# Two transfers for every weight block: a converting one into the first part, an adding one onto its negative

## The chip, the core and the metric

The kernel runs on one core of a Trainium2 chip. The metric is device time in microseconds (us), the median of the runs shown. The core has a matrix engine (PE; PEld is its weight load), a vector engine (DVE), an activation engine (ACT), a general engine (POOL), a sync engine (SP) that here only issues transfers, and 16 DMA engines that carry out what SP, ACT and POOL issue. Each engine works through its own instructions in order.

## The reference

The program is two transformer blocks on 512 tokens of width 1024, in f32. The first has a chunked state-space branch (SSD) of eight groups of heads, a banded attention, a gate and an MLP; the second has a parallel mixer, an attention to a memory and an MLP. What matters here is that nearly all of the work is products with weight matrices, such as

```python
proj = h @ w_in[l]
f = jnp.square(jax.nn.relu(h @ w_mlp_in[l])) @ w_mlp_out[l]
```

with the inner dimension of such a product 1024 or a multiple of it.

## The kernel before

**The products.** PE multiplies float32r, a rounded form of f32. To keep precision, a weight is held as two parts, `hi` (the weight rounded to float32r) and `lo` (what the rounding left), and an activation as two parts likewise. A product is then three matmuls: hi by hi, hi by lo and lo by hi (lines 266 to 268 in `cm`, channel-major; 284 to 286 in `tm`, token-major). For every 128 rows of weights the third matmul of `cm` is the first to need `lo`.

**The stream of blocks.** Weights come as a stream of some 140 blocks (`Unit`), nearly all of 1 MB: 128 partitions by 8 rows of 256 columns. `load` issues the transfer of a block into `raw`, from SP (line 129). `split` makes the parts, in two halves: ACT copies `raw` into `whi`, which rounds (line 140), and DVE subtracts `whi` from `raw` into `wlo` (line 141). `raw`, `whi` and `wlo` have two buffers each. `use` is called where a block's products begin: it sees that this block is split, and then `ahead` splits the next block and loads the one after that. So a transfer has about two blocks' time, and the split one block's time, before PE needs them.

**The order.** A tile framework records the program and arranges each engine's instructions by a schedule, so an instruction can stand earlier on its engine than the Python order says, but never runs before its inputs are there and its buffer is free.

**Around the change in the MLPs.** Each MLP has four quarters of four blocks of the first matrix (`f1`) and four of the second (`f2`). After each half of an `f1` block, ACT makes `relu` (line 1161) and its square `ua_h` (1162), POOL makes the square again in f32, `fsq` (1164), and DVE takes the difference as `ua_l` (1165). In the SSD stage POOL masks exponents (`e`, line 666), adds (`w`, 670; `xd`, 694 and 697) and issues the small transfers of `rh` and `lh` (561, 562, 626, 628), which go from f32 into float32r tiles.

Of the kernel before, what the change touches and what calls it, by code (L numbers as in the profile page):

```python
# [9 lines left out]
F32 = mybir.dt.float32  # L10
# [6 lines left out]
P = 128  # L17
# [5 lines left out]
WN = 2048  # L23
# [20 lines left out]
# columns of w_in  # L44
Z0, XBC0, DT0, Q0, K0, V0, G0 = 0, 2048, 6144, 6208, 7232, 7488, 7744
# columns of w_in_2
U0, VM0, OP0, IF0 = 0, 512, 1024, 1536

# columns of the packed constants
# [3 lines left out]
def packed_constants():  # L53
    """Constants that depend on shapes alone: the identity and its mirror image, the rotary
    frequencies, the one-hot of the relative position buckets, and the fixed rows of the products
    that make the exponents of the decays."""
# [11 lines left out]
    # rows 0..7 choose the chunk, rows 64..127 the pair that a token is in  # L68
# [4 lines left out]
    # rows 8..15 choose the head, rows 64..127 hide the pairs of tokens that a direction doesn't see  # L73
# [11 lines left out]
def body(ctx, tc, a, out, dbg=None):  # L85
# [26 lines left out]
    # ---------------------------------------------------------------- weights, as a stream of blocks  # L112
    win, win2 = a["w_in"][0], a["w_in_2"][0]

    class Unit:
        """A block of weights [128, kt, n], split into two parts of float32r whose sum it is."""

        def __init__(self, kt, n, loads, flat=None):
            self.kt, self.n, self.loads, self.flat = kt, n, loads, flat
            self.raw = self.hi = None  # L120
# [4 lines left out]
        def load(self):  # L125
            if self.raw is None:
                self.raw = self.view(wp.tile([P, WN], F32, name=nm("raw"), tag="raw", bufs=2))
                for dst, src in self.loads:
                    self.last = nc.sync.dma_start(out=dst(self.raw), in_=src)

        def split(self):
            if self.hi is None:
                self.load()
                self.hi = self.view(wp.tile([P, WN], F32R, name=nm("whi"), tag="whi", bufs=2))
                self.lo = self.view(wp.tile([P, WN], F32R, name=nm("wlo"), tag="wlo", bufs=2))
                n = self.flat or self.n
                for c in range(0, n, max(P, n // 2)):
                    e = min(n, c + max(P, n // 2))
                    sl = (slice(None), slice(c, e)) if self.flat else (slice(None), slice(None), slice(c, e))
                    A.copy(self.hi[sl], self.raw[sl])  # L140
                    V.tensor_tensor(out=self.lo[sl], in0=self.raw[sl], in1=self.hi[sl].bitcast(F32), op=ALU.subtract)  # L141
# [11 lines left out]
    def use(key, lag=False):  # L153
        """The unit; the next one is split at once or, with lag, where ahead() says."""
# [5 lines left out]
    def ahead(key, *behind):  # L160
        """The next unit being split, behind the given instructions, and the one after it on its way."""
# [9 lines left out]
    def evac_first(key, evac, *args):  # L171
        """evac, with the next unit's split behind the first of it on each engine."""
# [78 lines left out]
    # ---------------------------------------------------------------- helpers  # L251
    def cm(key, act, evac, parts=1):
        """Steps of a channel-major product: evac(j, psum) for each 128 columns of the unit, each in
        one step or more."""
# [19 lines left out]
    def tm(key, act, evac, ntile=NT):  # L274
        """Steps of a token-major product: evac(t, psum) for each 128 tokens."""
# [20 lines left out]
    def weave(main, side):  # L296
        """The steps of both lists, each list spread evenly."""
# [13 lines left out]
    def split_from(src, hi, lo, gain=None):  # L311
        """hi + lo = src * gain (a column of gains), both float32r."""
# [7 lines left out]
    def inv_rms(dst, ssq, n, width):  # L320
        """dst = (ssq / n + eps) ** -0.5 for [128, width] columns."""
# [3 lines left out]
    def token_sums(ssq, tag="t"):  # L325
        """Sums over the partitions of [128, 512], token-major in PSUM [128, 4]."""
# [5 lines left out]
    def bcast_tokens(r, tag="t"):  # L332
        """[128, 4] token-major -> PSUM [128, 512] on every partition."""
# [5 lines left out]
    # ---------------------------------------------------------------- persistent tiles  # L339
# [17 lines left out]
    # ---------------------------------------------------------------- block 1, first norm  # L357
# [12 lines left out]
    # the tensor engine's clock is at its full rate when the first inputs are here  # L370
# [34 lines left out]
    # ---------------------------------------------------------------- parameters, as columns  # L405
# [34 lines left out]
    # ---------------------------------------------------------------- dt and the decays  # L440
# [14 lines left out]
    # what the products for the exponents take: see ssd_exponents  # L455
# [4 lines left out]
    def dt_evac(_, po):  # L460
        """Rows (half, direction, head), two chunks of tokens in each half."""
# [17 lines left out]
        # cumulative sums of dt * a in each chunk, forwards and backwards  # L479
# [13 lines left out]
        # cs in two float32r parts, by way of DRAM, where the heads of a group are one row  # L493
# [8 lines left out]
        # the logarithm of dt, less cs, in two parts too  # L502
# [11 lines left out]
        # token-major: exp(cs) and dt * exp(tot - cs)  # L514
# [14 lines left out]
        def late():  # L529
# [8 lines left out]
            # the decay over a whole chunk, on every partition; step k takes chunk k and chunk 3 - k  # L538
# [25 lines left out]
    # ---------------------------------------------------------------- block 1, SSD branch  # L564
# [22 lines left out]
    class Group:  # L587
        """The SSD branch of one group of four heads."""
# [5 lines left out]
        # products, convolution and layouts  # L594
# [27 lines left out]
        # rows of the products for the exponents  # L622
# [32 lines left out]
        def exponents(self, c):  # L655
            """dt[s] exp(cs[l] - cs[s]) of both directions: cs[l] comes from rows 0..7,
# [1092 lines left out]
```

## Time and profile before

| | |
|---|---|
| median of 3 runs | 1943.59 us (1941.83 to 1944.87) |
| span of the profiled execution | 1939.5 us |
| PE busy | 1868.0 us (96%) |
| DVE / ACT / POOL busy | 1083.4 / 856.8 / 482.8 us |
| DMA queue of SP | 24.8% of the 16 engines' span |

The span runs from the first to the last instruction of the profiled execution; the page gives no other time of that execution. The difference of span and median, 4.1 us, is what lies around the span. A matmul's end is modelled, since matmuls are pipelined, so the distance from one matmul's start to the next is what one costs. Timeline rows give the start, then the duration, in us.

### The profile page before, as it was taken

How to read it: one execution, taken by the hardware profiler on the slowest of the kernel's cores; microseconds unless marked ns; L12 is line 12 of the kernel's file. 1: busy time of each engine (PE TensorE's matmuls, PEld its weight loads, DVE VectorE, ACT ScalarE, POOL GpSimd, SP SyncE). 2: the span in 40 equal slices, each digit the busy share in tenths (PEclk: the TensorE clock that was granted, in tenths of full speed). 3: DMA queues.
4: the chain of work that ended last, by engine and by line, in shares of the span. 5: the costliest groups of instructions: out<-in, count | busy, mean ns of one | idle time of the engine just before them, and what ended most of it. 6: DMA issues, size and time to landing. Idle time of an engine off the chain costs nothing. (4 is left out here: it accounts for less than half of the span.)

```text
span 1939.5 us, 24660 instructions
## 1 busy us (share of the span) xinstructions
PE 1868.0 (96%) x9685; PEld 1541.4 (79%) x9685; DVE 1083.4 (56%) x1751; ACT 856.8 (44%) x1397; POOL 482.8 (25%) x530
## 2 busy tenths in 40 slices
PE   8989999999999999998999999989999999999999
PEld 6878778887887777887888888888877778888887
DVE  7767773777555654537334334667567763334543
ACT  5655652755335665345332323444453543323231
POOL 1544450444202221233011202322110431111020
PEclk9999999999999999999999999999999999999999
DMA  6222122221222221333333332322111213232322
GB/s 174 68 67 67 45 67 87 67 67 44 82 94 82 82 78 66 119 122 109 98 109 98 101 94 89 114 73 74 51 45 65 87 44 108 90 107 87 109 87 65
DMA packets 169377, 164.10 MB, mean 85 GB/s; under 512 B 8742, under 2 KB 165101, under 8 KB 169262
## 3 DMA queue, kind: packets, MB, share of 16 engines
q1 hardware_dynamic: 157322, 151.03, 24.8%
q10 hardware_dynamic: 9444, 9.89, 1.6%
q0 software_dynamic: 2496, 1.61, 0.3%
q8 instruction: 76, 1.25, 0.3%
q14 instruction: 39, 0.32, 0.1%
HBM read 158.26 MB, written 4.23 MB: 84 GB/s over the span
## 5 line engine op out<-in xcount | busy, mean ns | idle before, releaser
L141 DVE TENSOR_TENSOR wlo<-raw,whi 128x1024 fp32r<-128x1024 f32 (+2 forms) x285 | 374.9, 1329 | 277.8 <-ACT whi L140 275.4
L140 ACT CAST whi<-raw 128x1024 fp32r<-128x1024 f32 (+2 forms) x285 | 288.3, 1029 | 408.9 <-PE psg L267 381.1
L266 PE MATMUL psg<-hh,whi 128*128 128x512 f32 (+1 forms) x1016 | 403.0, 397 | 0.8 <-DVE hl L318 0.8
L267 PE MATMUL psg<-hl,whi 128*128 128x512 f32 (+1 forms) x1016 | 400.7, 394 | 0.0
L268 PE MATMUL psg<-hh,wlo 128*128 128x512 f32 (+1 forms) x1016 | 399.3, 393 | 0.0
L266 PE MATMUL psg<-ua_h,whi 128*128 128x512 f32 x800 | 316.5, 396 | 0.5 <-DVE xT L1562 0.5
L267 PE MATMUL psg<-ua_l,whi 128*128 128x512 f32 x800 | 313.4, 392 | 0.0
L268 PE MATMUL psg<-ua_h,wlo 128*128 128x512 f32 x800 | 312.3, 390 | 0.0
L266 PEld LDWEIGHTS psg<-hh,whi 128*128 128x128 f32 (+1 forms) x1016 | 191.0, 188 | 40.5 <-issue 1.2
L268 PEld LDWEIGHTS psg<-hh,wlo 128*128 128x128 f32 (+1 forms) x1016 | 190.7, 188 | 39.7
L267 PEld LDWEIGHTS psg<-hl,whi 128*128 128x128 f32 (+1 forms) x1016 | 190.8, 188 | 38.1 <-DVE hl L315 0.4
L1164 POOL TENSOR_TENSOR fsq<-relu 128x512 f32<-128x512 f32 x64 | 80.9, 1264 | 507.9 <-ACT relu L1161 434.5
L266 PEld LDWEIGHTS psg<-ua_h,whi 128*128 128x128 f32 x800 | 150.1, 188 | 35.4 <-DVE xT L1562 2.4
L267 PEld LDWEIGHTS psg<-ua_l,whi 128*128 128x128 f32 x800 | 150.3, 188 | 32.3 <-DVE ua_l L1165 1.2
L268 PEld LDWEIGHTS psg<-ua_h,wlo 128*128 128x128 f32 x800 | 150.2, 188 | 30.7
L284 PE MATMUL psg<-whi,hh 128*128 128x256 f32 x416 | 121.5, 292 | 2.7 <-ACT sz L608 2.7
L286 PE MATMUL psg<-whi,hl 128*128 128x256 f32 x416 | 121.8, 293 | 0.0
L285 PE MATMUL psg<-wlo,hh 128*128 128x256 f32 x416 | 120.5, 290 | 1.0 <-DVE wlo L141 1.0
L986 POOL TENSOR_TENSOR ssq<-ssq,sq 128x512 f32<-128x512 f32 x42 | 66.4, 1582 | 117.0 <-ACT sq L985 116.0
L1165 DVE TENSOR_TENSOR ua_l<-fsq,ua_h 128x512 fp32r<-128x512 f32 x64 | 47.3, 739 | 79.2 <-POOL fsq L1164 79.2
L284 PEld LDWEIGHTS psg<-whi,hh 128*128 128x128 f32 x416 | 81.5, 196 | 5.9 <-ACT sz L608 4.0
L285 PEld LDWEIGHTS psg<-wlo,hh 128*128 128x128 f32 x416 | 81.4, 196 | 1.6 <-DVE wlo L141 1.2
(560 smaller groups left out, 2910.4 us busy)
## 6 DMA issues: line engine op xcount, KB each, us to landing
raw<-in_w_in_dram SPq DMA_DIRECT2D x37, 1024.0 KB
raw<-in_w_ff_dram SPq DMA_DIRECT2D x32, 1024.0 KB
raw<-in_w_mlp_in_dram SPq DMA_DIRECT2D x16, 1024.0 KB
raw<-in_w_mlp_out_dram SPq DMA_DIRECT2D x16, 1024.0 KB
raw<-in_w_in_dram SPq DMA_DIRECT2D x16, 512.0 KB
raw<-in_w_ssd_out_dram SPq DMA_DIRECT2D x8, 1024.0 KB
raw<-in_w_attn_out_dram SPq DMA_DIRECT2D x4, 1024.0 KB
raw<-in_w_o_dram SPq DMA_DIRECT2D x4, 1024.0 KB
```

The costliest lines, as they stand in the source:

```text
L140: A.copy(self.hi[sl], self.raw[sl])
L141: V.tensor_tensor(out=self.lo[sl], in0=self.raw[sl], in1=self.hi[sl].bitcast(F32), op=ALU.subtract)
L266: T.matmul(o, lhsT=u.hi[:, k, c:e], rhs=xh[k], start=k == 0, stop=False)
L267: T.matmul(o, lhsT=u.hi[:, k, c:e], rhs=xl[k], start=False, stop=False)
L268: T.matmul(o, lhsT=u.lo[:, k, c:e], rhs=xh[k], start=False, stop=k == u.kt - 1)
L284: T.matmul(o, lhsT=xh[k][:, tk], rhs=u.hi[:, k, 0 : u.n], start=k == 0, stop=False)
L285: T.matmul(o, lhsT=xh[k][:, tk], rhs=u.lo[:, k, 0 : u.n], start=False, stop=False)
L286: T.matmul(o, lhsT=xl[k][:, tk], rhs=u.hi[:, k, 0 : u.n], start=False, stop=k == u.kt - 1)
L986: G.tensor_tensor(out=self.t, in0=self.t, in1=q, op=ALU.add)
L1164: G.tensor_tensor(out=f, in0=r, in1=r, op=ALU.mult)
L1165: V.tensor_tensor(out=ua_l[:, m, :], in0=f, in1=ua_h[:, m, :].bitcast(F32), op=ALU.subtract)
```

## The change

The tile `raw` is gone. `load` now issues a transfer straight into `whi`, from POOL, with the conversion to float32r done by the transfer. `split` has ACT write the negative of `whi` into `wlo` (two halves, as before), and then issues from POOL a second transfer of the same weights that adds onto `wlo`. DVE's subtraction is gone. `whi` and `wlo` have three buffers each in place of two, so that the six buffers of a block's size stay six. All else in the diff is comments taken out; lines behind the class move by two.

```diff
         def load(self):
-            if self.raw is None:
-                self.raw = self.view(wp.tile([P, WN], F32, name=nm("raw"), tag="raw", bufs=2))
+
+            if self.hi is None:
+                self.hi = self.view(wp.tile([P, WN], F32R, name=nm("whi"), tag="whi", bufs=3))
                 for dst, src in self.loads:
-                    self.last = nc.sync.dma_start(out=dst(self.raw), in_=src)
+                    self.last = nc.gpsimd.dma_start(out=dst(self.hi), in_=src)
 
         def split(self):
-            if self.hi is None:
+
+            if self.lo is None:
                 self.load()
-                self.hi = self.view(wp.tile([P, WN], F32R, name=nm("whi"), tag="whi", bufs=2))
-                self.lo = self.view(wp.tile([P, WN], F32R, name=nm("wlo"), tag="wlo", bufs=2))
+                self.lo = self.view(wp.tile([P, WN], F32R, name=nm("wlo"), tag="wlo", bufs=3))
...
-                    A.copy(self.hi[sl], self.raw[sl])
-                    V.tensor_tensor(out=self.lo[sl], in0=self.raw[sl], in1=self.hi[sl].bitcast(F32), op=ALU.subtract)
+                    A.activation(self.lo[sl], self.hi[sl].bitcast(F32), AF.Copy, scale=-1.0)
+                for dst, src in self.loads:
+                    nc.gpsimd.dma_start(out=dst(self.lo), in_=src, accum_op=ALU.add)
```

POOL's queue in the first MLP, `f1` blocks of a later quarter, before. It holds the squares alone; the loads are on SP.

```order
L1164 TENSOR_TENSOR fsq_1355_8239<-relu_1354_8236 128x512 [waits Activation_49,Pool_49]
L1164 TENSOR_TENSOR fsq_1358_8270<-relu_1357_8267 128x512 [waits Activation_49,Pool_49]
L1164 TENSOR_TENSOR fsq_1364_8309<-relu_1363_8306 128x512 [waits Activation_49,Pool_49]
L1164 TENSOR_TENSOR fsq_1367_8340<-relu_1366_8337 128x512 [waits Activation_49,Pool_49]
L1164 TENSOR_TENSOR fsq_1373_8379<-relu_1372_8376 128x512 [waits Activation_49,Pool_49]
```

The same place after. Line 143 is the adding transfer, line 130 the converting one; the first number behind a name is the buffer's own, in the order in which the program takes them: `whi_1336` and `wlo_1343` are one block, `whi_1344` and `wlo_1351` the next.

```order
L143 DMA wlo_1335_8612<-in_w_mlp_in_dram 128x8x256 [waits DMASW5_49,PE_49,Activation_49]
L130 DMA whi_1336_8616<-in_w_mlp_in_dram 128x8x256 [waits DMASW6_49,PE_49]
L1166 TENSOR_TENSOR fsq_1334_8609<-relu_1333_8606 128x512 [waits Activation_49,Pool_49]
L1166 TENSOR_TENSOR fsq_1339_8646<-relu_1338_8643 128x512 [waits Activation_49,Pool_49]
L143 DMA wlo_1343_8680<-in_w_mlp_in_dram 128x8x256 [waits DMASW7_49,PE_49,Activation_49]
L130 DMA whi_1344_8684<-in_w_mlp_out_dram 128x8x256 [waits DMASW0_49,PE_49]
L1166 TENSOR_TENSOR fsq_1342_8677<-relu_1341_8674 128x512 [waits Activation_49,Pool_49]
L1166 TENSOR_TENSOR fsq_1347_8714<-relu_1346_8711 128x512 [waits Activation_49,Pool_49]
L143 DMA wlo_1351_8748<-in_w_mlp_out_dram 128x8x256 [waits DMASW1_49,PE_49,Activation_49]
L130 DMA whi_1352_8752<-in_w_mlp_out_dram 128x8x256 [waits DMASW2_49,PE_49]
```

Both transfers of a block now stand between the squares, and the converting transfer of a block stands right behind the adding one of the block before it.

ACT's queue at the same place, before:

```order
L140 CAST whi_1359_8273<-raw_1352_8209 128x8x128 [waits DMAHW0_49,PE_49]
L1161 ACTIVATE relu_1357_8267<-psg_1356_8242 128x512 [waits DVE_49,PE_49]
L140 CAST whi_1359_8273<-raw_1352_8209 128x8x128
L1162 ACTIVATE ua_h_74<-relu_1357_8267 128x512 [waits Activation_49]
L1161 ACTIVATE relu_1363_8306<-psg_1362_8281 128x512 [waits DVE_49,PE_49]
L1162 ACTIVATE ua_h_74<-relu_1363_8306 128x512 [waits Activation_49]
```

and after:

```order
L141 ACTIVATE wlo_1343_8680<-whi_1336_8616 128x8x128 [waits DMASW7_49,DMASW4_49]
L1163 ACTIVATE relu_1338_8643<-psg_1337_8618 128x512 [waits DVE_49,PE_49]
L141 ACTIVATE wlo_1343_8680<-whi_1336_8616 128x8x128
L1164 ACTIVATE ua_h_74<-relu_1338_8643 128x512 [waits Activation_49]
L1163 ACTIVATE relu_1341_8674<-psg_1340_8649 128x512 [waits DVE_49,PE_49]
L1164 ACTIVATE ua_h_74<-relu_1341_8674 128x512 [waits Activation_49]
```

The two halves now enclose the `relu` of a block's first half instead of that of its second half, and the wait for PE (a `whi` buffer to be free) is replaced by waits for transfers.

## Rows read from the trace of the kernel before

**Rows 1.** Page, part 1: busy time, share of the span, instructions of each engine.
```profile
PE 1868.0 (96%) x9685; PEld 1541.4 (79%) x9685; DVE 1083.4 (56%) x1751; ACT 856.8 (44%) x1397; POOL 482.8 (25%) x530
```

**Rows 2.** Who waited for whom: us in total, times, longest.
```profile
ACT whi L140 <- PE psg L267: 381.1, 79, 9.3
DVE wlo L141 <- ACT whi L140: 275.4, 127, 11.1
...
SPq L129 <- DVE wlo L141: 1463.4, 121, 39.2
```

**Rows 3.** Groups by line and form: count | busy us, mean ns | idle before, releaser.
```profile
L141 DVE TENSOR_TENSOR wlo<-raw,whi 128x1024 fp32r<-128x1024 f32 x275 | 368.6, 1354 | 274.5 <-ACT whi L140 274.3
...
L140 ACT CAST whi<-raw 128x1024 fp32r<-128x1024 f32 x275 | 283.6, 1048 | 408.5 <-PE psg L267 381.1 <-issue 11.4 <-PE pse L1226 9.6
...
L712 PE MATMUL pst<-ident,sz 128*128 128x128 f32 x60 | 12.7, 312 | 10.5 <-DVE ua_l L318 5.8 <-DVE sz L707 4.7
```

**Rows 4.** Timeline of ACT over one block of the first MLP.
```profile
998.36 1.05 ACT L140 CAST whi<-raw 128x1024 fp32r<-128x1024 f32 x1 [3.95 <-PE psg L267]
999.31 0.59 ACT L1161 ACTIVATE relu<-psg 128x512 f32<-128x512 f32 x1
...
1009.24 1.05 ACT L140 CAST whi<-raw 128x1024 fp32r<-128x1024 f32 x1 [3.95 <-PE psg L267]
```

**Rows 5.** One load of 1 MB: SP's timeline row, then the stretch; last columns clock, DMA share, GB/s.
```profile
1002.68 0.37 SPq L129 DMA_DIRECT2D raw<-in_w_mlp_out_dram  x1
...
1003.00:1008.00 5.00, 5.00 (x24) 4.14 (x23) 0.94 (x2) 1.23 (x2) 1.04 (x1) 1.00 0.63 210
```

**Rows 6.** Lines 561, 562, 626: POOL's issue, ns min/median/max, and us to landing.
```profile
L561 POOL DMA_DIRECT2D rh<-in_consts_dram x2: 540/666/792, 12.2 to 14.1; - x2
...
DMA to landing us min/median/max: 3.2/5.2/7.2
...
L562 POOL DMA_DIRECT2D lh<-in_consts_dram x2: 537/549/561, 13.5 to 14.6; - x2
...
DMA to landing us min/median/max: 6.6/7.2/7.8
...
L626 POOL DMA_DIRECT2D rh<-csd x16: 507/552/641, 42.5 to 424.5; - x16
...
DMA to landing us min/median/max: 1.9/2.0/3.0
```

**Rows 7.** POOL's timeline, then POOL's DMA queue at 13.5 to 15 and 15 to 16.5 us.
```profile
12.20 0.79 POOL L561 DMA_DIRECT2D rh<-in_consts_dram  x1
...
13.51 0.56 POOL L562 DMA_DIRECT2D lh<-in_consts_dram  x1
...
q0 software_dynamic: 143, 0.26, 73.0%
...
q0 software_dynamic: 2, 0.00, 0.5%
```

**Rows 8.** Line 140 by stage: ACT busy (instructions; two are a block), clock, DMA share, GB/s.
```profile
0.00:560.00 560.00, 71.18 (x69) 0.98 0.26 79
560.00:857.00 297.00, 42.97 (x42) 1.00 0.28 90
...
1205.00:1530.00 325.00, 41.56 (x46) 0.99 0.23 73
```

**Rows 9.** Stretches around a pause of PE: PE, PEld, DVE, ACT, POOL, clock, DMA share, GB/s.
```profile
262.00:264.00 2.00, 0.59 (x3) 0.19 (x2) 2.00 (x2) 1.97 (x4) 1.92 (x4) 1.00 0.00 0
264.00:270.00 6.00, 5.45 (x21) 4.66 (x22) 5.38 (x11) 3.25 (x6) 2.03 (x5) 0.72 0.55 175
```

**Rows 10.** SP's first loads, behind those of x.
```profile
0.79 1.85 SPq L361 DMA_DIRECT2D acc<-in_x_dram  x4
2.68 11.09 SPq L129 DMA_DIRECT2D raw<-in_w_in_dram  x4
```

More of the change, by code (lines that the diff above doesn't have):

```diff
@@ L119, in __init__ @@
             self.kt, self.n, self.loads, self.flat = kt, n, loads, flat
-            self.raw = self.hi = None
+            self.hi = self.lo = None
         def view(self, t):
```

## The prediction

> **What bounds the kernel now.** I read the page's busy times first, then the waits, then one block of the first MLP in the timeline. PE is busy 96% of the span, DVE 56% [rows 1]. The split is done while PE works: DVE spends 368.6 us on the subtractions and ACT 283.6 us on the casts [rows 3], but the casts mostly wait for PE to free a `whi` buffer (381.1 us in 79 waits), the subtractions for the casts, and SP's loads for the subtractions (1463.4 us) [rows 2]. Everything around the weights therefore waits for PE, and PE for almost nothing. One MLP block takes 1009.24 - 998.36 = 10.88 us, from one cast that PE releases to the next [rows 4]; that is PE's own pace, and the number that the new supply of blocks has to meet. A load of 1 MB needs only 3.2 us of the DMA engines: in the 5 us from 1003, in which one such load passes, they are busy for a share of 0.63 [rows 5].
>
> **What the change takes away.** DVE loses 285 subtractions, about 375 us of busy time. Since PE hardly waits for DVE, little comes of it: the clearest group of such waits, the transposes of line 712 in the SSD stage, idles 10.5 us in all [rows 3]. I credit 10 us, with 0 and 25 us as ends. SP loses its loads, which cost nothing, since their waits stood on an engine with nothing else to do in those stages.
>
> **What it adds, and the new chain.** Each block now needs a converting transfer, ACT's negation (two halves, as long as the casts: 1.05 us each, [rows 4]) and an adding transfer, both transfers from POOL. On POOL the converting transfer of block k+1 stands right behind the adding transfer of block k, and the adding transfer waits for ACT's negation, which waits for the converting transfer of its own block to land. The third buffer of `whi` does not break this: whatever the buffers allow, POOL comes to load k+1 only after it has issued the adding transfer of k. So there is a loop, and its length is the least time in which blocks can come:
>
> 1. from the issue of the adding transfer to its first bytes: 1.3 us (POOL's 12.20 issue moves its first bytes after 13.5, [rows 7]);
> 2. the adding transfer itself, Ta;
> 3. the converting transfer, which goes through the same queue behind it: 3.2 us, as a load takes now [rows 5]; POOL's present transfers from f32 into float32r moved 0.26 MB in the 1.5 us from 13.5 at 73% of the engines [rows 7], 0.26 / (1.5 x 0.73) = 0.24 MB per engine-filled us, which is 4.4 us a block while another queue was also active, so 3.2 to 4.4, and I take 3.2;
> 4. to its landing: 0.5 us (3.2 us from issue to landing for that 0.26 MB, less 1.3, less some 1.4 of moving, [rows 6, 7]);
> 5. the negation: 2 x 1.05 us, and in `f1` blocks the `relu` that stands between its halves, 0.6 us [rows 4];
> 6. 0.1 us for the semaphore to POOL.
>
> Without Ta that is 7.2 us, and 7.8 us in `f1` blocks. To this comes the making of descriptors: a block has 1024 rows of 1 KB, where POOL's largest transfer of before has 128. POOL's issue takes 0.552 us with 8 rows and 0.666 us with 128 [rows 6], so 1 ns a row, and 1.0 us for a block; for the second transfer it lies beside the first one's moving. By the landing times instead, 3.2 against 2.0 us [rows 6], less 0.8 us for the bytes, 0.4 us for 120 rows, it would be 3.4 us. I take 1.0, the issue being the direct measure, and keep 0 and 3.4.
>
> Ta is the large unknown; no row shows an adding transfer. It reads the weights and also what lies in `wlo`, and writes once. The lowest that I allow is a plain load, 3.2 us. I take twice that, 6.4 us, since twice the bytes are read. The upper end is 10.2 us: POOL's four transfers of 256 KB were issued from 12.20 to 14.6 and the last landed 7.8 us after its issue, so that 1 MB took 10.2 us [rows 6, 7]. The Trainium skill (Collectives: The Full Stack, section "The bandwidth ceiling: the fold count and why AG ≠ RS ≠ AR") puts the slowness of an adding DMA down to its two reads for each write and not to the addition, about half the rate of a copy; by that page Ta would be an estimated 6.4 us too and the sum the same; no run here shows it yet.
>
> **The sum.** With Ta = 6.4 the loop is 7.8 + 1.0 + 6.4 = 15.2 us in `f1` blocks and 14.6 us in `f2` blocks, against 10.88 us that PE needs. PE then waits for `wlo` at the third matmul of each block.
> - The two MLPs: 32 x (15.2 - 10.9) + 32 x (14.6 - 10.9) = 138 + 118 = 256 us.
> - 560 to 857 us has 42 half-block casts, 21 blocks at 14.1 us, and 1205 to 1530 us has 23 blocks at 14.1 us [rows 8]. The mean is just under the loop, but some of these blocks follow each other at the MLP's pace and others at twice that; between +0.5 and +4 us each I take 2.5: 44 x 2.5 = 110 us.
> - 0 to 560 us has 34.5 blocks at 16.2 us [rows 8], longer than the loop. POOL's masks and additions now stand behind transfers that wait. I take 1 us each, 35 us, with ends 0 and 3.
> - The start: the first blocks now share the engines with x, where they stood behind it [rows 10]: +3 us, between 0 and 5.
> - DVE's relief: -10 us.
>
> Sum: 256 + 110 + 35 + 3 - 10 = 394 us, on the span of 1939.5 us: 2333 us, and with the 4.1 us that lie between this span and the median, 2338 us; I say 2340.
>
> What is costed at nothing: POOL's squares `fsq` behind the transfers, since `ua_l` is only needed in `f2`, up to half a block later; if that cover is gone, it adds to the first `f2` block of each of eight quarters a few us. The DMA engines carry 3.2 + 6.4 = 9.6 us per block, below the loop, so their throughput does not add. The clock is costed at nothing too: PE's pauses of 3 to 4 us a block may bring it down, as a pause around 264 did: PE was busy 0.59 of the 2 us before, and the granted clock of the next 6 us was 0.72 in the mean [rows 9]. That is 3.4 us at the lower level (1.2 GHz), and costs PE half of it, 1.7 us; 10.9 + 1.7 = 12.6 us is still below the loop of 14.6.
>
> **Rivals.**
> - *The adding transfer costs no more than a load.* Ta = 3.2 and few ns for descriptors: the loop is 10.4 us (`f2`) to 11.0 (`f1`), even with PE. Then the MLPs lose 32 x 0.1 = 4 us, the other stages about 1 us a block at most (0 to 78 us), the start 3: 1944 + 4 + 40 + 3 - 10 = about 1980 us, between 1950 and 2100. For it: the loads use a quarter of the engines' time, so nothing is crowded. Against: it must read twice.
> - *POOL's transfers are slow to start and slow to move.* The transfer of line 562 was issued at 13.51, but POOL's queue moved 2 packets between 15 and 16.5 us [rows 7], so its first bytes came 3.0 us after the issue, not 1.3, while SP's queue was busy and DVE ran without a pause. With 3.0 in place of 1.3 and Ta = 10.2 the loop is 7.8 + 1.7 + 10.2 = 19.7 us (`f1`) and 19.1: 32 x 8.8 + 32 x 8.2 + 44 x 5.5 + 34.5 x 3.5 = 907, so 2844 us; with 3.4 us for descriptors on top some 3300. The Trainium skill (SBUF — State Buffer, section "Who interferes with whom") has a rule to this effect, that a DVE instruction in a two-port mode blocks POOL's descriptor making, and that SP's transfers are immune; whether that was the cause at 15 us the trace does not tell, since SP's queue was full as well.
> - *Not slower at all: the supply is hidden and DVE's relief shows.* This decides at Ta of 3.1 us or less with no descriptor time, where the loop is no longer than PE's 10.88 us in both kinds of block. The third buffers then keep a block in hand, and the relief of 10 to 25 us is net: 1920 to 1935 us. For it: PE idles 10.5 us on line 712 alone. Against: Ta would have to be below a plain load.
>
> **How the numbers follow.** The forecast (2150 to 2550) has a chance of 0.50, the cheap adding transfer 0.17, the slow one (2550 to 3300) 0.24, a gain 0.05, and no change (relief against small losses) 0.04. Differences under 0.2%, about 4 us, cannot be told from none here. The likeliest is 2340 us. The range has to reach into both neighbours: 1970 leaves out the gain and a part of the cheap case, about 0.1, and 2850 leaves out the worst of the slow case, about 0.1. Faster 0.05, same 0.04, slower 0.91.
>
> **What would show it.** Right: DVE's busy time down by some 370 us and no faster for it; PE's waits put down to the adding transfer's `wlo`; MLP blocks 14 to 16 us apart and equal to the distance of POOL's adding transfers; the DMA share in the MLPs at about 9.6 / 15 = 0.65; the SSD stage hardly longer. Wrong: an adding transfer that takes 3 us, or more than 10; a POOL that is itself the bound, its issue instructions lasting several us; a PE that falls to the lower clock and is late for that reason rather than for the supply; or a stage other than the MLPs that loses most.

## The result, and the profile after

The changed kernel takes 2274.4 us (median of four runs, 2272.2 to 2281.6) where the kernel before takes 1943.8 us: a ratio of 1.171, 95% interval 1.169 to 1.173. The forecast was 2340 us with a range of 1970 to 2850, so the direction, the mechanism and the range held, and the size was 66 us too large. The profiled run took 2272.2 us with a span of 2270.2 us, so the stages below are compared span against span (1939.5 before).

The page of the changed kernel, parts 1 and 3 (busy time, share, instructions; then the packets, MB and share of POOL's DMA queue), answers to [rows 1]:

```profile
PE 1954.8 (86%) x9685; PEld 1595.5 (70%) x9685; DVE 751.0 (33%) x1466; ACT 846.7 (37%) x1392; POOL 813.4 (36%) x840
...
q0 software_dynamic: 302368, 293.73, 71.8%
```

DVE lost 332 us of work and the kernel became 331 us longer. Who waits now (us in total, times, longest), against [rows 2]:

```profile
POOL wlo L143 <- ACT wlo L141: 560.2, 78, 14.0
...
ACT wlo L141 <- DMA whi<-in_w_ff_dram: 266.1, 27, 13.9
...
PEld psg L268 <- ACT relu L1163: 93.3, 24, 9.3
```

Before, the casts waited for PE. Now POOL's adding transfers wait for ACT's negation and the negation for the converting transfer. PE waits for what the adding transfer brings, or for a `relu` that stands behind a waiting negation on ACT. One turn of this loop in the first MLP: POOL's timeline, ACT's, and PE's waits in this turn and in the next (start, us, what; in brackets the idle time before and its releaser).

```profile
1162.13 1.54 POOL L143 DMA_DIRECT2D wlo<-in_w_mlp_out_dram  x1 [11.06 <-ACT wlo L141]
1163.03 1.55 POOL L130 DMA_DIRECT2D whi<-in_w_mlp_in_dram  x1
1176.25 1.54 POOL L143 DMA_DIRECT2D wlo<-in_w_mlp_in_dram  x1 [11.68 <-ACT wlo L141]
1177.15 1.55 POOL L130 DMA_DIRECT2D whi<-in_w_mlp_in_dram  x1
1190.85 1.53 POOL L143 DMA_DIRECT2D wlo<-in_w_mlp_in_dram  x1 [12.15 <-ACT wlo L141]
...
1173.95 2.01 ACT L141 ACTIVATE wlo<-whi 128x1024 fp32r<-128x1024 f32 x2 [12.21 <-DMA whi<-in_w_mlp_in_dram]
...
1171.02 0.47 PE L270 MATMUL psg<-ua_h,wlo 128*128 128x512 f32 x1 [1.57 <-DMA wlo<-in_w_mlp_out_dram]
...
1185.58 0.47 PE L270 MATMUL psg<-hh,wlo 128*128 128x512 f32 x1 [3.39 <-DMA wlo<-in_w_mlp_in_dram]
```

The same turn in stretches; the last three columns are the granted clock, the DMA engines' share and GB/s:

```profile
1162.00:1164.50 2.50, 2.50 (x12) 2.06 (x11) 0.69 (x1) 0.00 (x0) 2.37 (x2) 1.00 0.04 9
1164.50:1170.00 5.50, 4.95 (x22) 3.75 (x20) 0.69 (x1) 0.00 (x0) 0.07 (x1) 1.00 1.21 184
1170.00:1173.10 3.10, 2.08 (x9) 1.76 (x10) 0.00 (x0) 0.00 (x0) 0.00 (x0) 1.00 1.49 346
1173.10:1176.20 3.10, 3.10 (x16) 2.54 (x15) 0.00 (x0) 2.01 (x2) 0.00 (x0) 1.00 0.02 2
```

Read these two together and the loop is there link by link: issue to first bytes 2.4 us (1162.13 to 1164.5, hardly any bytes move); the adding transfer 5.5 us at 184 GB/s; the converting transfer, issued long before, 3.1 us at 346 GB/s; landing and ACT's start 0.85 us (1173.1 to 1173.95); the negation 2.0 us; 0.3 us to POOL's next adding transfer. Together 14.1 us, the distance of the two L143 rows. In the last stretch almost nothing is transferred (2 GB/s), while PE works on what is left.

Where the 330 us went, by operations that all kernels have, in us per stage: the SSD stage's transposes (line 712 of before; the expectations call the first of them the first decay step), the additions to the residual stream behind the attention and behind the first MLP (line 1005, first and last), the query factors of the attention to the memory (1654, last) and the output copies (1703, last). "Block" is the mean distance of blocks inside the MLPs, from the first `relu` of the second quarter to the last of the fourth, 19.5 blocks, in the first and the second MLP:

| kernel | to first 712 | from it to last 712 | attention | MLP 1 | mixer | MLP 2 | block |
|---|---|---|---|---|---|---|---|
| before | 106.1 | 404.6 | 367.1 | 388.2 | 288.7 | 379.5 | 10.94, 10.92 |
| changed | 127.9 | 414.2 | 411.4 | 498.9 | 326.9 | 485.2 | 14.43, 14.46 |
| no adding transfer | 125.3 | 399.1 | 368.8 | 382.5 | 286.2 | 379.4 | 10.81, 10.77 |
| second transfer plain | 123.2 | 406.7 | 374.9 | 426.6 | 306.8 | 421.3 | 12.34, 12.39 |
| two halves | 126.6 | 417.3 | 403.7 | 468.9 | 325.2 | 452.4 | 13.39, 13.38 |
| load first | 118.4 | 405.5 | 388.8 | 426.0 | 329.2 | 409.6 | 11.55, 11.31 |
| four `whi`, load in front | 125.4 | 407.6 | 381.5 | 432.2 | 333.4 | 411.2 | 11.52, 11.62 |
| four `whi`, load behind | 122.5 | 403.5 | 387.2 | 434.1 | 339.3 | 410.0 | 11.75, 11.39 |

The two MLPs lost 216 us, attention and mixer 83, everything up to the end of the SSD stage 31.

### The profile page after: what moved, and what is told of

Read it like the earlier page. It is cut to its first block, busy times and chain, and to the rows that moved or that the text cites. A ratio compares the mean times of both kernels' runs of the same rounds, so it can differ in the third digit from the quotient of the medians.

```text
span 2270.2 us, 24625 instructions
## 1 busy us (share of the span) xinstructions
PE 1954.8 (86%) x9685; PEld 1595.5 (70%) x9685; DVE 751.0 (33%) x1466; ACT 846.7 (37%) x1392; POOL 813.4 (36%) x840
## 5 line engine op out<-in xcount | busy, mean ns | idle before, releaser
L141 ACT ACTIVATE wlo<-whi 128x1024 fp32r<-128x1024 f32 (+2 forms) x285 | 288.8, 1034 | 932.9 <-DMA whi<-in_w_ff_dram 266.1
L268 PE MATMUL psg<-hh,whi 128*128 128x512 f32 (+1 forms) x1016 | 424.4, 418 | 88.0 <-ACT relu L1163 71.7
L270 PE MATMUL psg<-hh,wlo 128*128 128x512 f32 (+1 forms) x1016 | 412.1, 406 | 16.7 <-DMA wlo<-in_w_mlp_in_dram 8.6
L269 PE MATMUL psg<-hl,whi 128*128 128x512 f32 (+1 forms) x1016 | 413.5, 407 | 0.2 <-DVE hl L317 0.2
L268 PE MATMUL psg<-ua_h,whi 128*128 128x512 f32 x800 | 323.7, 405 | 33.1 <-ACT acc L1171 14.5
L270 PE MATMUL psg<-ua_h,wlo 128*128 128x512 f32 x800 | 318.5, 398 | 20.9 <-DMA wlo<-in_w_mlp_out_dram 10.2
L268 PEld LDWEIGHTS psg<-hh,whi 128*128 128x128 f32 (+1 forms) x1016 | 200.0, 197 | 139.3 <-ACT relu L1163 79.3
L270 PEld LDWEIGHTS psg<-hh,wlo 128*128 128x128 f32 (+1 forms) x1016 | 199.8, 197 | 63.5 <-issue 15.2
L269 PEld LDWEIGHTS psg<-hl,whi 128*128 128x128 f32 (+1 forms) x1016 | 200.4, 197 | 41.5 <-DVE hl L317 1.0
L143 POOL DMA_DIRECT2D wlo<-in_w_in_dram x55 | 89.9, 1672 | 160.2 <-ACT wlo L141 109.4
L288 PE MATMUL psg<-whi,hl 128*128 128x256 f32 x416 | 122.5, 295 | 0.0
L143 POOL DMA_DIRECT2D wlo<-in_w_ff_dram x32 | 49.9, 1558 | 183.6 <-ACT wlo L141 169.7
## 6 DMA issues: line engine op xcount, KB each, us to landing
whi<-in_w_mlp_out_dram POOLq DMA_DIRECT2D x16, 1024.0 KB, 10.9
```

The costliest lines, as they stand in the source:

```text
L141: A.activation(self.lo[sl], self.hi[sl].bitcast(F32), AF.Copy, scale=-1.0)
L143: nc.gpsimd.dma_start(out=dst(self.lo), in_=src, accum_op=ALU.add)
L268: T.matmul(o, lhsT=u.hi[:, k, c:e], rhs=xh[k], start=k == 0, stop=False)
L269: T.matmul(o, lhsT=u.hi[:, k, c:e], rhs=xl[k], start=False, stop=False)
L270: T.matmul(o, lhsT=u.lo[:, k, c:e], rhs=xh[k], start=False, stop=k == u.kt - 1)
L288: T.matmul(o, lhsT=xl[k][:, tk], rhs=u.hi[:, k, 0 : u.n], start=False, stop=k == u.kt - 1)
```

## The experiments

The theory: the time is set by a chain that closes on itself through POOL's queue (load k+1 stands behind the adding transfer of k, which waits for a negation, which waits for load k). The rivals: the adding transfers cost what they cost on the DMA engines and on POOL, in whatever order they stand; or the second transfer is no dearer for adding, and two transfers with their starts are the loss. The expectations say TensorE, VectorE, ScalarE, GpSimd and SyncE for PE, DVE, ACT, POOL and SP.

**No adding transfer.**

```diff
-                for dst, src in self.loads:
-                    nc.gpsimd.dma_start(out=dst(self.lo), in_=src, accum_op=ALU.add)
```

> The adding transfer is left out, so the second part holds only the negative of the first: part of the computation is missing. Theory (the loss is a chain load - negation - adding transfer - next load of about 14.3 us against TensorE's 10.88 us a block, plus a late start): without the adding transfer nothing holds the next load back, so a block is paced by TensorE again; what stays is the start, where the converting loads share the DMA engines with x (the first 128 us of the changed kernel are 21.8 us late, about 11 of them by the first product). 1943.8 + 11 to 22 - up to 10 for VectorE's relief: 1952 us, range 1940 to 1965. Rival (the loads from GpSimd's queue, or the queue itself in front of the squares and the small transfers, cost most of it): 2100 us or more.

Measured: 1948.1 us, ratio 1.002 (1.0009 to 1.003). With the first transfers on POOL and ACT's negation both still in place, nearly everything is back; blocks come at 10.8 us. What stays is the start (125.3 us to the first transpose against 106.1), and 12.1 us of those 19.2 are regained behind it, 5.5 in the SSD stage and 5.7 in the first MLP. That is the size put down to DVE's relief (10 us), but it did not come where the prediction looked for it. PE's waits for DVE at the transposes of line 712, 10.5 us before, are 11.9 us here and 14.3 us in the changed kernel (line 714 there; the largest rows, this run first):

```profile
PE pst L712 <- DVE sz L707: 11.3, 8, 1.8
...
PE pst L714 <- DVE sz L709: 12.1, 10, 1.9
```

A run below in which DVE still subtracts gets back 12 us in the SSD stage, also after a late start. Whether any of the 12.1 us is DVE's relief was not isolated.

**The second transfer plain.**

```diff
-                    nc.gpsimd.dma_start(out=dst(self.lo), in_=src, accum_op=ALU.add)
+                    nc.gpsimd.dma_start(out=dst(self.lo), in_=src)
```

> The second transfer stays where it is and moves the same bytes, but overwrites the negative instead of adding to it, so the second part holds the rounded weight: the computation is changed. Theory: the transfer takes 3.1 us as the converting one does, instead of about 5.6, so the loop is 14.3 - 2.5 = 11.8 us, 0.9 us over TensorE's 10.88 instead of 3.4. Of the 308 us lost behind the start 82 stay: 1943.8 + 22 + 82 = 2047 us, range 2010 to 2090. Rival (the transfer is no slower for adding; the loop is long by two transfers, their starts and their landings alone): 2274 us, same as the changed kernel.

Measured: 2056.1 us, ratio 1.057 (1.055 to 1.059). This run gives the price of adding in place of overwriting: the same program order and the same 304 MB read from the memory. It does not tell the addition from the second read that goes with it. POOL's timeline, and the stretches of one turn:

```profile
1171.36 0.94 POOL L143 DMA_DIRECT2D wlo<-in_w_mlp_out_dram  x1 [9.25 <-ACT wlo L141]
1172.30 0.88 POOL L130 DMA_DIRECT2D whi<-in_w_mlp_out_dram  x1
...
1173.00:1179.50 6.50, 6.50 (x31) 5.37 (x30) 0.69 (x1) 0.00 (x0) 0.18 (x1) 1.00 1.57 322
1179.50:1182.50 3.00, 3.00 (x15) 2.49 (x14) 0.69 (x1) 2.01 (x2) 0.00 (x0) 1.00 0.02 2
```

Both transfers now pass in 6.5 us at 322 GB/s, 3.2 us each, against 5.5 + 3.1. And the issue itself takes 0.94 us instead of 1.54, so that first bytes come 1.65 us after its start, not 2.4. Together some 3 us off the loop in this turn; over the MLPs the block went from 14.43 to 12.34 us (the profiled run took 2066.4 us). Of the 330 us, 218 are the adding. The rest is the loop of two plain transfers, which is still longer than PE's block, and the late start (17 us). The rival, for which this run had to stay at 2274, is out.

**The load first.** The same work, but load k+1 stands ahead of the adding transfer of k on POOL (`split` issues its adding transfer behind the loads that it is given):

```diff
+        for u in stream[i + 2 : i + 3]:
+            u.load()
...
-                u.split()
-        for u in stream[i + 2 : i + 3]:
-            u.load()
+                u.split(stream[i + 2 : i + 3])
```

> All work is kept; on GpSimd's queue the load of the next block but one now stands ahead of the adding transfer, not behind it. Theory: the load no longer waits for the negation, and its landing no longer waits behind the adding transfer of its predecessor. What is left is: buffer free at the start of a block, issue and first bytes 2.3, load 3.1, adding transfer 5.6, landing 0.8, semaphore 0.1 = 11.9 us against 10.88, 1.0 us a block over instead of 3.4: 308 x 1.0 / 3.4 = 91, with the start's 22: 2057 us, range 1990 to 2110. Rival (it is not the chain but what the transfers and their descriptors cost on DMA engines and GpSimd, whatever the order): 2274 us.

Measured: 2081.0 us, ratio 1.070 (1.067 to 1.073). Order alone, with every transfer as dear as before, takes away 193 of the 330 us, so the resource rival is out as the main cause. POOL's timeline in the first MLP:

```profile
1061.37 0.95 POOL L130 DMA_DIRECT2D whi<-in_w_mlp_out_dram  x1 [2.14 <-PE psg L273]
...
1063.33 1.61 POOL L146 DMA_DIRECT2D wlo<-in_w_mlp_out_dram  x1
...
1072.53 0.94 POOL L130 DMA_DIRECT2D whi<-in_w_mlp_out_dram  x1 [2.52 <-PE psg L273]
...
1074.47 1.61 POOL L146 DMA_DIRECT2D wlo<-in_w_mlp_out_dram  x1
```

The load now waits for PE to free a buffer, and the adding transfer no longer waits for anything: blocks at 11.2 us here, 11.3 to 11.6 in the mean, where 11.9 was worked out. The time is 24 us over the expected one, inside the range, and that excess lies outside the MLPs, which lost 68 us where 64 were worked out. The mixer lost 40 us and gained nothing (329.2 us against 326.9), for the new order has a wait of its own there:

```profile
1376.10 0.98 POOL L130 DMA_DIRECT2D whi<-in_w_in_dram  x1 [9.09 <-PE psg L291]
1377.07 1.60 POOL L146 DMA_DIRECT2D wlo<-in_w_in_dram  x1
...
PE psg L290 <- DMA wlo<-in_w_in_dram: 12.5, 2, 8.4
```

A load without a buffer held POOL for 9.1 us, with an adding transfer behind it that could have gone, and PE waited for that one (last row: PE's largest wait of the stage).

**Two halves.** Negation and adding transfer in two halves by slices, the first transfer issued when the first half is negated:

```diff
+                    for k in (0, KT // 2):
+                        sl = (slice(None), slice(k, k + KT // 2))
+                        A.activation(self.lo[sl], self.hi[sl].bitcast(F32), AF.Copy, scale=-1.0)
+                        nc.gpsimd.dma_start(out=self.lo[sl], in_=self.loads[0][1][sl], accum_op=ALU.add)
```

> All work is kept, the order of the changed kernel too; the negation and the adding transfer of each block with eight slices are done in two halves by slices, the first half's transfer being issued when the first half is negated. Theory (the negation's 2.0 us and the start of the adding transfer are links of the chain): the adding transfer starts 1.05 us earlier and its first issue is shorter, so the loop goes from 14.3 to 12.6 to 13.2 us, and of 308 us behind the start 95 to 150 go: 2155 us, range 2110 to 2200. Rival (a transfer's fixed start is paid twice, or the two halves take longer than one whole): 2274 us or more.

Measured: 2204.2 us, ratio 1.134 (1.132 to 1.136), just above the range: 70 us came back where 95 to 150 were expected. The negation is a link of the loop, as it must be for this to gain anything; the block is 13.39 us. Part of what ate the rest is POOL's issue:

```profile
1169.93 2.58 POOL L142 DMA_DIRECT2D wlo<-in_w_mlp_in_dram  x2 [10.25 <-ACT wlo L141]
1171.54 1.88 POOL L130 DMA_DIRECT2D whi<-in_w_mlp_in_dram  x1
```

Two issues of 512 rows take 2.58 us, one of 1024 rows 1.54. I had put down half the rows at half the price. The two halves also took 6.0 us to move in this turn (1172 to 1178 us), against 5.5 us for the whole.

**Four buffers for `whi`, two for `wlo`.** First with the load still in front of the adding transfer, then with the load behind it but one block further ahead:

```diff
-                self.hi = self.view(wp.tile([P, WN], F32R, name=nm("whi"), tag="whi", bufs=3))
+                self.hi = self.view(wp.tile([P, WN], F32R, name=nm("whi"), tag="whi", bufs=4))
...
-                self.lo = self.view(wp.tile([P, WN], F32R, name=nm("wlo"), tag="wlo", bufs=3))
+                self.lo = self.view(wp.tile([P, WN], F32R, name=nm("wlo"), tag="wlo", bufs=2))
```

The second of them starts from the changed kernel, and issues these loads behind the adding transfer of block i + 1:

```diff
-        for u in stream[i + 2 : i + 3]:
+            for u in stream[i + 2 : i + 4]:
```

> All work is kept. As in the kernel with the load first (2081 us), and four buffers for the first part, two for the second: a load no longer waits for TensorE to leave a buffer in front of an adding transfer, but the negation waits until TensorE has left the block before last. Theory: the chain inside a block is negation 2.1, first bytes 2.3, adding transfer 5.6, landing 0.5, semaphore 0.1 = 10.6 us, with a relu between the halves 11.2, against 10.88: the two MLPs lose 0 to 13 us each instead of 38 and 30; the mixer, which lost 40 us with the load first by waiting there for adding transfers that stood behind a load without a buffer, loses 10 to 25. With 14 by the end of the SSD stage and 5 to 15 in the attention: 2010 us, range 1975 to 2060. Rival (what is left in the kernel with the load first is the price of the adding transfers on DMA engines and GpSimd, not a chain): 2081 us or more.

> All work is kept; four buffers for the first part and two for the second, the adding transfer ahead of the load again, but the load one block further ahead: no negation waits for the load issued right behind the adding transfer before it. Theory: the chain that is left begins where TensorE leaves a block: negation with relu and square between 2.9 (2.1 in the second product), semaphore 0.1, first bytes 2.3, adding transfer 5.6, landing 0.6 = 11.5 to 11.9 us in the first product, 10.7 in the second, against 10.88. So each MLP loses 10 to 17 us, not the 44 of the run that has the load's 3.1 us in front: 2101 - 2 x 29 = 2043 us, less up to 10 in the mixer, range 2000 to 2070. Rival (the loss that is left is the price of the adding transfers on DMA engines and GpSimd, whatever the order): 2090 us or more.

Measured: 2101.0 us (ratio 1.081, 1.079 to 1.083) and 2099.8 us (1.082, 1.080 to 1.084). Both expectations failed, and by the totals the rival would have it. The timeline of the second one says otherwise (POOL, then ACT's negation and PE):

```profile
1168.13 1.58 POOL L143 DMA_DIRECT2D wlo<-in_w_mlp_out_dram  x1 [1.68 <-ACT wlo L141]
...
1178.90 1.58 POOL L143 DMA_DIRECT2D wlo<-in_w_mlp_out_dram  x1 [1.54 <-ACT wlo L141]
...
1190.16 1.57 POOL L143 DMA_DIRECT2D wlo<-in_w_mlp_out_dram  x1 [8.78 <-ACT wlo L141]
...
1164.67 0.60 ACT L1167 ACTIVATE relu<-psg 128x512 f32<-128x512 f32 x1 [4.18 <-PE psg L274]
...
1177.00 0.50 PE L274 MATMUL psg<-ua_h,wlo 128*128 128x512 f32 x1 [1.00 <-DMA wlo<-in_w_mlp_out_dram]
```

PE leaves the block before last at 1164.7, the adding transfer is issued 3.5 us later (two negation halves with `relu` and square between them), and PE has it at 1177.0, 8.9 us after the issue: 12.3 us for a block that is split during `f1`, and PE waited 1.0 us for it. During `f2`, with only 2.0 us of negation ahead, the issues stand 10.9 to 11.3 us apart. So a chain is still there, one that two buffers of `wlo` close. In the second run I had it 0.4 to 0.8 us too short in `f1` and 0.2 to 0.6 us in `f2`; in the first I overlooked that the load's 3.1 us stand in front of the adding transfer after all, since both are released by the same event. In the first MLP of the second run, some 27 of the 46 us lost are PE's waits for adding transfers, and some 19 are longer matmuls at a granted clock of 0.97.

The larger part of the miss is outside the MLP blocks: attention and mixer lost 14 to 20 and 45 to 51 us. PE's waits in the second run's mixer name the adding transfers again, 40 us in all (largest row):

```profile
PE psg L291 <- DMA wlo<-in_w_in_dram: 18.4, 3, 7.1
```

The matmuls were 17 us longer there, at a granted clock of 0.92 (below). Why the adding transfers come late in the mixer was not tried, and stays open.

**The start.** The first two loads issued behind POOL's first step on x:

```diff
-    unit_of["dt"].load()
-    unit_of["bc", 0].load()
...
+        if t == 0:
+            with tc.issue_after(last.ins):
+                unit_of["dt"].load()
+                unit_of["bc", 0].load()
```

> All work is kept; the first two blocks' converting loads are issued behind GpSimd's first step on x, not at the program's start. Theory (of the 21.8 us lost before 128 us about 10 come from x sharing the DMA engines with these loads): x arrives as in the kernel before, the first product starts some 8 us earlier, and the first decay step of the SSD stage stands at about 119 instead of 127.9 us; all later steps move with it: 2266 us, range 2260 to 2272. Rival (the start is held by the queue of GpSimd, with the small transfers behind megabytes, not by x): 2274 us, or later by what the loads come later.

Measured: 2270.6 us, ratio 1.168 (1.166 to 1.170) against 1.171, 4 us where 8 were expected. x does arrive as before, and the first product starts at 18.9 instead of 26.0 us. But PE had been busy for half of the 7 us before, its granted clock was 0.55 from 20 to 25 us, and the first transpose only moves from 127.9 to 125.1. What it waits for are the exponents of the decays (line 663 of before), which begin at 50.0 us in the kernel before, at 78.5 in the changed one and at 73.3 here. They need `csd`, the sums of the decays, which SP writes to the memory and POOL fetches into `rh`, and `gld`, which POOL fetches into `lh`. SP's and POOL's rows in the kernel before, then in the changed one with a row of ACT:

```profile
37.71 2.65 SPq L500 DMA_DIRECT2D csd<-w  x4
...
42.53 1.03 POOL L626 DMA_DIRECT2D rh<-csd  x2 [27.41 <-DMA csd<-w]
...
45.34 1.13 POOL L628 DMA_DIRECT2D lh<-gld  x2 [1.78 <-DMA gld<-w]
```

```profile
50.21 2.67 SPq L502 DMA_DIRECT2D csd<-w  x4
...
57.87 1.19 POOL L628 DMA_DIRECT2D rh<-csd  x2
...
64.57 1.13 POOL L630 DMA_DIRECT2D lh<-gld  x2 [3.88 <-issue]
...
40.43 1.06 ACT L141 ACTIVATE wlo<-whi 128x1024 fp32r<-128x1024 f32 x1 [6.63 <-DMA whi<-in_w_in_dram]
```

`csd` is 12.5 us late. ACT, which makes its parts, stands in front of them with a negation that waits 6.6 us for a transfer; its negations wait 21.0 us for transfers up to the first transpose, where the casts of before waited 2.8 us. That is less than half of the 28.5 us by which the exponents are late: POOL issues `rh` 15.3 and `lh` 19.2 us late, on a queue that now holds adding transfers too, so the rival (POOL's queue) is not out, and how the rest divides was not tried. The last experiment below, which brings the first three blocks in the old way, has the exponents at 48.7 and the first transpose at 109.5 us: 18 of the 21.8 us are the new supply of those blocks. The sharing with x explains 7 us of the late first product, and 3 of them reach the first transpose.

**One part alone, and mixtures.** The first part by a converting transfer from POOL, the raw block by SP, DVE subtracts, no adding transfer:

```diff
+                for dst, src in self.loads:
+                    nc.sync.dma_start(out=dst(self.raw), in_=src)
-                    A.activation(self.lo[sl], self.hi[sl].bitcast(F32), AF.Copy, scale=-1.0)
+                    V.tensor_tensor(out=self.lo[sl], in0=self.raw[sl], in1=self.hi[sl].bitcast(F32), op=ALU.subtract)
```

> One part of the change alone: the first part by a converting transfer from GpSimd's queue, the raw block by SyncE's queue as before, and VectorE subtracts; ScalarE's pass and the adding transfer are gone. Theory: no transfer waits for an engine's pass over what another one brought, so TensorE paces the blocks again; the two transfers of a block take 2 x 3.2 us of the DMA engines. The start stays late by 8 to 15 us, ScalarE's 284 us of casts give back little since TensorE was 96% busy: 1950 us, range 1935 to 1970. Rival (two transfers for each block, or GpSimd's issues, are the loss): 2100 us or more.

Measured: 1962.4 us, ratio 1.009 (1.008 to 1.011). Two transfers for each block, 2 MB from the memory, cost 1%, so it is not their number that costs 17%. Its SSD stage was 12 us shorter from the first transpose to the last (392.5 us). Two mixtures tried to keep that, with the old supply for the first three blocks and from the first MLP on; the first has three buffers of `whi` and one of `raw`, the second two of each:

> A mixture, all work kept: the first three blocks and all from the first MLP on come as in the kernel before (one load by SyncE, ScalarE casts, VectorE subtracts); the other blocks of the SSD stage and the attention have the first part by a converting transfer and the raw block by SyncE, VectorE subtracts. Theory: with that source of the first part the SSD stage gained 12 us between its first decay step and its end (392.5 against 404.6 us), which a late start of 12 us ate; with the first blocks from SyncE the start is as before and the gain stays: 1932 us, range 1924 to 1946. Rival (that gain was only the late start being caught up with): 1944 us or more.

> All work kept; the mixture of the run before, with two buffers each for raw block, first and second part, as in the kernel before. Theory: the mixture lost 14 us at the start because ScalarE's cast of the second block waited for a raw buffer (a wait of 3.4 us on the load of raw, ending at 32.3 us), and 9 + 6 + 5 us in the first MLP, the mixer and the second MLP for the same lack; with two raw buffers these are as in the kernel before, and the 12 us gained between the first decay step and the end of the SSD stage stay: 1932 us, range 1924 to 1946. Rival (that gain is only a late start being caught up with): 1944 us, range 1940 to 1950.

Measured: 1965.5 us (1.011, 1.009 to 1.013) and 1966.7 us (1.013, 1.011 to 1.014). In the first, one raw buffer cost 14 us at the start and some 20 behind it; the SSD stage was again 12 us shorter. In the second, the start is 3 us late (109.5) and everything from the first MLP on (388.3, 288.5, 379.5) is as before, but the SSD stage took 409.8 us and the attention 386.7, 5 and 20 more than before. The 12 us are not there without a late start or a third buffer; which of the two it was these runs don't separate. The attention's loss can be read from DVE's waits there (us, times, longest):

```profile
DVE wlo L148 <- DMA whi<-in_w_in_dram: 30.7, 11, 5.4
...
DVE wlo L148 <- DMA whi<-in_w_attn_out_dram: 18.5, 4, 10.7
```

With two buffers the converting transfer can only start when PE leaves a block, and DVE, in whose queue the softmax stands behind the subtraction, waits for it; PE's waits for that softmax grew from 0.5 to 10.2 us. This is read from the waits, and no run tried it alone. No version found here beats the kernel before.

## Why the prediction was right, and where it was off

**The loop** was right in kind: it closes where the prediction closed it, blocks are 14 to 15 us apart, equal to the distance of the adding transfers, and six edits that cut or shorten it brought back 70 to 326 us. Link by link, in a block of the second product:

| link, us | predicted | measured |
|---|---|---|
| issue to first bytes, with the descriptors | 2.3 | 2.4 |
| adding transfer (Ta) | 6.4 | 5.5 |
| converting transfer | 3.2 | 3.1 |
| landing | 0.5 | 0.85 |
| negation | 2.1 | 2.0 |
| semaphore | 0.1 | 0.3 |

The largest miss is **Ta**, the time of the adding transfer, by 0.9 us, of which landing and semaphore gave back 0.55.

**The start of the adding transfer** came out right, 2.3 and 2.4 us, but by luck. The 1.0 us for 1024 rows was worked out at 1 ns a row from a median of two issues (0.540 and 0.792 us), though the same group of rows has another transfer of 128 rows at 0.549 us, no longer than one of 8 rows. The plain second transfer shows 0.94 us for its issue and 1.65 us to first bytes, so rows are cheaper than 1 ns; the other 0.75 us come with the adding, for which the prediction had no term.

**Ta by its rule.** The plain transfer of the same megabyte takes 3.2 us and the adding one 5.5, 1.7 times as long. The rule of the Trainium skill that was cited (Collectives: The Full Stack, "The bandwidth ceiling: the fold count and why AG ≠ RS ≠ AR": two reads for each write, about half a copy's rate) gives 2 times; the page has it for the reduce step of a collective and puts it down to the second read, not to the addition. The runs put the factor lower, and do not tell read from addition.

**The sum.** MLPs: 256 predicted, 216 measured, since the block grew by 3.5 us and not by 4.3 and 3.7. Attention and mixer: 110 against 83; the 2.5 us a block, chosen between 0.5 and 4, should have been 1.9. Up to the end of the SSD stage: 35 + 3 against 31. DVE's relief: 10 us credited, which no run isolates, and PE's waits on line 712, from which it was read, grew. So 40, 27 and 7 us too much, less the 10 credited: 64 us, 40 of it in the MLPs.

**The start** was mis-sized, and only by luck inside the sum: 3 us were put down for x sharing the engines and 35 for the blocks of the SSD stage, and it was 21.8 by the first transpose and 9.6 after it. The step that failed is the one that let the first blocks' transfers weigh only on x. It did not ask what ACT has behind a negation that waits.

That is also missing from the MLPs' description. The prediction had PE wait for `wlo` in each block; in `f1` blocks it waits mostly for ACT instead. PE's waits in the first MLP, then ACT's timeline and PE's:

```profile
PE psg L268 <- ACT relu L1163: 39.8, 12, 8.3
...
PE psg L270 <- DMA wlo<-in_w_mlp_in_dram: 8.6, 3, 3.5
...
1203.01 1.06 ACT L141 ACTIVATE wlo<-whi 128x1024 fp32r<-128x1024 f32 x1 [12.45 <-DMA whi<-in_w_mlp_in_dram]
1203.97 0.58 ACT L1163 ACTIVATE relu<-psg 128x512 f32<-128x512 f32 x1
...
1204.61 0.79 PE L268 MATMUL psg<-hh,whi 128*128 128x512 f32 x1 [8.34 <-ACT relu L1163]
```

The `relu` that frees a PSUM bank (the buffer into which PE adds up a product) stands behind a negation that waits 12.5 us for the next block's load. It cost little beyond the loop, being inside it: blocks are 14.4 us apart all the same. But it is the reason that the profile puts 93 us of the idle time of PE's weight loads down to `relu`.

**The clock**, costed at nothing, was indeed covered in the MLPs: PE's matmuls got longer there (granted clock 0.92, PE busy 407.6 us over 498, where it was 378.1 before) and the loop is longer still. By the busy times it is not covered in the mixer. The mixer of the kernel with the load first, and of the kernel before (columns as above, PE's busy time first):

```profile
1339.00:1668.00 329.00, 293.26 (x1640) 241.57 (x1641) 162.29 (x411) 139.04 (x268) 101.96 (x109) 0.92 0.51 103
```

```profile
1266.00:1555.00 289.00, 274.07 (x1631) 223.70 (x1631) 197.36 (x451) 137.26 (x270) 62.34 (x66) 0.99 0.20 64
```

The same matmuls took 19 us longer there, which may be as much as half of that stage's 40; no run isolates it. In the changed kernel's mixer the clock was 0.95 and PE was busy 14 us longer; how much of the stage's 38 us this was has not been isolated either.

**The rivals.** That the adding transfer costs no more than a load: out, and the plain second transfer shows what it would have given, 2056 us and not 1980, since the links around it were a little longer than that rival had them. Slow to start and slow to move: 2.4 us to first bytes and 5.5 us of moving, where it needed 3.0 and 10.2. Not slower at all: no run was faster, and even without the adding transfer the time was 1948 us, where this rival needed 1920 to 1935. The DMA share in the MLPs, 0.65 foretold, was 0.83 and 0.75: the adding phase alone counts 1.21 at 184 GB/s.

## What to carry to other kernels

Before a step is handed from an engine to a transfer, draw the cycle in which the transfer waits for an engine's pass over what another transfer of the same queue brought, and add up its links; if it exceeds the block's work, the cycle sets the pace. The third buffer did not help here; another order on the queue gave back 193 of 331 us. Look behind each new wait on an in-order engine for what others need from it: here a negation in front of a `relu`, and in front of the first decays. A transfer that adds is priced by itself, in its issue as well as in its moving.

## What was not expected of the hardware

POOL's issue of a transfer costs by kind and by piece: 0.9 us for a converting one with 1024 rows (1.55 us right behind an adding one), 1.55 us for an adding one with 1024 rows, and still 1.3 us for an adding one with 512.

DVE's instructions grew where POOL was busy. Line 707, a multiplication of 128 x 256, takes 0.348 us in the median of the kernel before. In the run without the adding transfer four of them in a row took 4.1 us; DVE's row, then POOL's beside it:

```profile
124.49 4.09 DVE L707 TENSOR_SCALAR sz<-sz,ssg 128x256 f32<-128x256 f32 x4 [1.80 <-POOL ssg L323]
...
124.40 0.57 POOL L626 DMA_DIRECT2D rh<-csd  x1
124.99 0.75 POOL L666 TENSOR_SCALAR_AFFINE_SELECT e<-e 128x512 f32<-128x512 f32 x1
125.71 0.57 POOL L628 DMA_DIRECT2D lh<-gld  x1
126.30 1.27 POOL L670 TENSOR_TENSOR w<-e,e 128x512 f32<-128x512 f32 x1
```

In the changed kernel the same line (L709 there) has a median of 0.715 us. So DVE's busy time fell by 332 us and not by 375; other lines grew too. The Trainium skill (SBUF — State Buffer, "Who interferes with whom") states that GpSimd and DVE share a pair of ports, that some DVE instructions can take it, a multiplication by a scalar among them, and that whoever has it locks the other out for a whole instruction. The row agrees in kind; which of POOL's instructions it was here, the masks or the issues, the trace does not tell. POOL's transfers alone are not enough for it: with the raw block from SP and as many converting transfers from POOL, the median is 0.349 us.
